# Plus-only weight sums, two of them by an accumulating DMA, and more pieces with seven block products

## The chip, the cores and the metric

One NeuronCore of a Trainium2 chip runs the kernel in one launch. The metric is device time in microseconds (us), the median of several executions; less is better.

## What is computed

One decoder layer on 256 tokens, model width 2048, all in float32. The change lies in the last stage, a dense SwiGLU network with 5632 hidden columns, and in the weights' preparation for it. Cut to that stage, the reference is:

```python
D_MODEL, SEQ = 2048, 256
D_FF = ((8 * D_MODEL // 3 + 255) // 256) * 256      # 5632
...
h2 = _rms(x, norm2_g[l])
a = jax.nn.silu(jnp.einsum('bsd,df->bsf', h2, w_gate[l])) * jnp.einsum('bsd,df->bsf', h2, w_up[l])
x = x + jnp.einsum('bsf,fd->bsd', a, w_down[l])
...
return _rms(x, final_norm_g)
```

Ahead of it stand an RMS norm, a wide projection, a spatial gate and a retention on its columns, and an output projection; none of these is changed, except that the sums of `h2` (below) are made while the output projection runs.

## The kernel before

**Three products for one.** Every float32 operand of a matrix product is split into a rounded part `hi` and the rest `lo`, and a product is made as hi·hi + hi·lo + lo·hi: three matmuls of 128x128 by 128x512 on TensorE (PE), all recorded at line 45. For the weights the split is made on the fly (`split`, lines 47 to 55): ScalarE (ACT) casts `hi` (L53), then VectorE (DVE) subtracts to get `lo` (L54). `hi` and `lo` have four buffers each, 1024 columns wide; the loaded weights `raw` have three buffers of 1 MB (128 x 2048 float32), filled by SyncE's DMA queue (SP) in the order of the program.

**Pieces.** Gate and up are computed in 11 groups `j` of 512 hidden columns. A group runs through 8 pieces `p`; a piece holds 256 rows of the weights, as two halves of 128 rows, for 512 columns of gate and 512 of up. So a piece is a product of 2x2 blocks: two row blocks of tokens and two halves on the left, two halves and {gate, up} on the right. The down projection has the same form: two groups `c` of 22 pieces, with two blocks of 512 output columns in the place of gate and up. `quad` (from line 499) runs the pieces of one group.

**Classic and seven.** A classic piece makes 8 block products, 24 matmuls. A piece in `seven` makes 7 by Winograd's form of Strassen's scheme, 21 matmuls, and pays with sums: of the left blocks (`sums_of`, made once for `h2`) and of the right blocks, the weights, for each piece (`pair_seven`, from line 475). Four of the seven products have accumulators of their own, numbered 1, 5, 7 and 6, in the PSUM pool `sm`; they run through all seven-pieces of a group, and after the last one ACT and DVE combine them (`mixed`, L533 to L537), to be added to the four classic banks in `acc`. Before, `SEVEN_GU = (1, 3, 5)`: three of the 8 pieces in each group of gate and up are seven-pieces, and none in down.

**Sums of weights.** A raw tile holds the four blocks b12, b11, b22, b21 beside each other. Before, DVE makes b12-b11 and b12-b22 in one instruction of 1024 columns (L484), then b22 minus the first (L487) and b21 minus that (L488). ACT and DVE then split four tiles: `plain` (b11, b22), `one` (the two differences), `last` (b21, 512 columns) and `two` (the other two sums).

**What sets the order.** Each engine runs its instructions in order. The order on an engine is made when the program is built, from the written order, the buffers and estimated durations; it can stand apart from the written one by some instructions. A buffer comes free when its last reader is done: a `raw` buffer with the last `lo` or sum made from it, a `hi` or `lo` buffer with the last matmul that reads it. `finish_up` (from line 575) adds banks and sums, and applies the gate (L582, L583, L587, L588); `turn_a` transposes the result on PE (L598) one group later, at the piece that `todo` names.

Of the kernel before, what the change touches and what calls it, by code (L numbers as in the profile page):

```python
# [15 lines left out]
P = 128  # L16
# [14 lines left out]
SEVEN_GU = (1, 3, 5)  # L31
# [4 lines left out]
def block_kernel(ctx: ExitStack, tc: tile.TileContext, a: dict, out: bass.AP):  # L36
# [386 lines left out]
    def sums_of(x11, x12, x21, x22, dst):  # L423

        t = ff.tile([P, 4, P], F32, name="sums", bufs=1)
        nc.vector.tensor_tensor(out=t[:, 0, :], in0=x21, in1=x22, op=ALU.add)
        nc.vector.tensor_tensor(out=t[:, 1, :], in0=x21, in1=x11, op=ALU.subtract)
        nc.vector.tensor_tensor(out=t[:, 2, :], in0=t[:, 0, :], in1=x11, op=ALU.subtract)
        nc.vector.tensor_tensor(out=t[:, 3, :], in0=x12, in1=t[:, 2, :], op=ALU.subtract)
        nc.scalar.copy(dst[:, 0, :, :], t)  # L430
        nc.vector.tensor_tensor(out=dst[:, 1, :, :], in0=t, in1=dst[:, 0, :, :].bitcast(F32), op=ALU.subtract)

    def turn_x(c):
        for half in range(2):
# [41 lines left out]
    def pair_seven(src):  # L476
# [3 lines left out]
        b12, b22, b21 = raw[:, 0:NC], raw[:, 2 * NC:3 * NC], raw[:, 3 * NC:]  # L480
        t = big.tile([P, 4 * NC], F32, name=f"mT{next(odd) % 2}")
        t13, t24 = t[:, 0:2 * NC], t[:, 2 * NC:]
        (plain,) = split(raw[:, NC:3 * NC], 2 * NC, 2 * NC)
        nc.vector.tensor_tensor(  # L484
            out=t13.rearrange("p (b c) -> p b c", b=2), in0=b12.unsqueeze(1).broadcast_to([P, 2, NC]),
            in1=raw[:, NC:3 * NC].rearrange("p (b c) -> p b c", b=2), op=ALU.subtract)
        nc.vector.tensor_tensor(out=t24[:, 0:NC], in0=b22, in1=t13[:, 0:NC], op=ALU.subtract)  # L487
        nc.vector.tensor_tensor(out=t24[:, NC:], in0=b21, in1=t24[:, 0:NC], op=ALU.subtract)  # L488
        (one,) = split(t13, 2 * NC, 2 * NC)
        (last,) = split(b21, NC, NC)  # L490
        (two,) = split(t24, 2 * NC, 2 * NC)
# [12 lines left out]
    def quad(src, order, seven, left, forms, todo=(), apart=0):  # L504
# [6 lines left out]
        classic_left = [p for p in order if p not in seven]  # L511
# [240 lines left out]
```

## Time and profile before

| | |
|---|---|
| median of 3 executions | 1107.33 us (1106.61 to 1108.31) |
| the profiled execution, its own time | 1108.35 us |
| its span, first to last instruction | 1106.1 us |
| PE busy | 1088.6 us, 98% |
| DVE busy | 810.6 us, 73% |
| ACT busy | 570.2 us, 52% |
| POOL (GpSimd) busy | 55.0 us, 5% |
| moved by DMA | 217.64 MB, 197 GB/s over the span |

An engine's busy time is the time in which it had an instruction running; an instruction's duration includes its pipeline, so that two that follow each other overlap, and the distance from one start to the next is less than the duration. A chain of waits is followed back from the last instruction to what released it. A DMA's time to landing runs from its issue to its semaphore.

### The profile page before, as it was taken

What the parts mean: (1) busy time and instruction counts of PE and PEld (TensorE: products, weight loads), DVE (VectorE), ACT (ScalarE), POOL (GpSimd) and SP (SyncE); (2) the same over time, 40 slices, a digit from 0 to 9 for tenths busy, and PEclk for the clock granted to TensorE, in tenths of its full rate; (3) what the DMA queues carried; (4) which work ended last, traced back from release to release, by engine and by line L of the source; (5) the groups of instructions that cost most, each with busy time, mean ns of one, the idle gap of its engine ahead of it and who ended that gap; (6) DMA issues with size and microseconds to landing.
All of it is one profiled execution on the core that took longest, in us unless ns stands there. A gap on an engine that the chain in (4) does not pass through costs nothing.

```text
span 1106.1 us, 12891 instructions
## 1 busy us (share of the span) xinstructions
PE 1088.6 (98%) x4937; PEld 901.6 (82%) x4937; DVE 810.6 (73%) x1097; ACT 570.2 (52%) x664; POOL 55.0 (5%) x36
## 2 busy tenths in 40 slices
PE   8989999999999999999999999999999999999996
PEld 7868888888888888888888888888888888888885
DVE  6895458466556789889898898898899555575555
ACT  6623433444445556556555555655656454454443
POOL 0051014011000000000000000000000000020000
PEclk9999999999999999999999999999999999999998
DMA  9846554545555455655645555655556655555551
GB/s 353 329 139 235 190 189 156 189 152 190 190 188 184 166 185 193 224 183 197 213 174 193 221 190 190 205 196 208 190 191 231 225 190 190 190 190 192 194 185 76
DMA packets 32749, 217.64 MB, mean 197 GB/s; under 512 B 3760, under 2 KB 4144, under 8 KB 7088
## 3 DMA queue, kind: packets, MB, share of 16 engines
q1 hardware_dynamic: 32544, 215.78, 54.7%
q0 software_dynamic: 144, 1.05, 0.3%
q8 instruction: 38, 0.62, 0.2%
q14 instruction: 23, 0.19, 0.0%
HBM read 214.72 MB, written 2.10 MB: 196 GB/s over the span
## 4 chain that ended last, share of the span: by engine, by line
PE 95%; DVE 2%; DMA 1%; ACT 0%; SPq 0%; issue 0%; DVEq 0%; ACTq 0%
PE acc L45 84%; PE sm L45 9%; PE sm L598 1%; DMA raw<-in_w_in 1%; DVE lo L54 1%; PE sm L439 0%; PE sm L334 0%; ACT junk L218 0%; DVE rs_r L75 0%; DVE rs_w L74 0%; PE sm L380 0%; DVE work L254 0%; DVE x L653 0%; SPq L168 0%; DVE rs_w L73 0%
## 5 line engine op out<-in xcount | busy, mean ns | idle before, releaser
L45 PE MATMUL acc<-hi,hT 128*128 128x512 f32 x2484 | 786.6, 391 | 1.9 <-ACT hi L53 1.9
L54 DVE TENSOR_TENSOR lo<-raw,hi 128x1024 fp32r<-128x1024 f32 (+1 forms) x396 | 463.2, 1182 | 249.6 <-ACT hi L53 243.1
L53 ACT CAST hi<-raw 128x1024 fp32r<-128x1024 f32 (+1 forms) x396 | 395.5, 1009 | 441.0 <-PE acc L45 417.5
L45 PEld LDWEIGHTS acc<-hi,hT 128*128 128x128 f32 x2484 | 467.3, 188 | 98.4 <-ACT hi L53 2.3
L45 PE MATMUL acc<-lo,hT 128*128 128x512 f32 x1242 | 484.7, 390 | 4.1 <-DVE lo L54 4.1
L45 PEld LDWEIGHTS acc<-lo,hT 128*128 128x128 f32 x1242 | 233.7, 188 | 53.3 <-DVE lo L54 5.8
L54 DVE TENSOR_TENSOR lo<-mT,hi 128x1024 fp32r<-128x1024 f32 x66 | 80.6, 1220 | 16.1 <-ACT hi L53 16.1
L53 ACT CAST hi<-mT 128x1024 fp32r<-128x1024 f32 x66 | 69.6, 1055 | 30.3 <-DVE lo L54 17.0
L45 PE MATMUL acc<-hi,mT 128*128 128x512 f32 x256 | 80.1, 391 | 0.1
L45 PE MATMUL sm<-hi,h2s 128*128 128x512 f32 x198 | 71.8, 390 | 0.0
L45 PEld LDWEIGHTS acc<-hi,mT 128*128 128x128 f32 x256 | 48.1, 188 | 10.3 <-ACT mT L383 0.5
L45 PE MATMUL acc<-lo,mT 128*128 128x512 f32 x128 | 49.7, 389 | 0.0
L45 PEld LDWEIGHTS sm<-hi,h2s 128*128 128x128 f32 x198 | 37.1, 188 | 7.7
L484 DVE TENSOR_TENSOR mT<-raw 128x1024 f32<-128x1024 f32 x33 | 40.2, 1220 | 0.8 <-DMA raw<-in_w_gu 0.2
L45 PE MATMUL sm<-lo,h2s 128*128 128x512 f32 x99 | 38.5, 389 | 0.0
L619 POOL DMA_DIRECT2D hT<-in_gf x1 | 0.7, 717 | 598.9 <-DVE mT L582 598.9
L587 ACT ACTIVATE sg<-mT,rstd 128x512 f32<-128x512 f32 x22 | 15.9, 722 | 24.6 <-DVE mT L582 24.6
L631 DVE TENSOR_TENSOR hT<-af,hT 128x1024 fp32r<-128x1024 f32 x22 | 27.9, 1267 | 0.7 <-ACT hT L630 0.7
L45 PEld LDWEIGHTS acc<-lo,mT 128*128 128x128 f32 x128 | 24.0, 188 | 4.8
L45 PE MATMUL sm<-hi,hT 128*128 128x512 f32 x66 | 25.7, 389 | 0.0
L45 PE MATMUL acc<-hi,h2s 128*128 128x512 f32 x66 | 25.7, 389 | 0.0
L258 POOL TENSOR_TENSOR work<-work,gains 128x512 f32<-128x512 f32 x8 | 17.5, 2192 | 124.1 <-DVE work L254 62.1
(99 smaller groups left out, 551.8 us busy)
## 6 DMA issues: line engine op xcount, KB each, us to landing
raw<-in_w_gu SPq DMA_DIRECT2D x88, 1024.0 KB, 4.7
raw<-in_w_in SPq DMA_DIRECT2D x47, 1024.0 KB, 4.8
raw<-in_w_down SPq DMA_DIRECT2D x44, 1024.0 KB, 4.7
raw<-in_w_out SPq DMA_DIRECT2D x16, 1024.0 KB, 4.8
x<-in_x SPq DMA_DIRECT2D x2, 1024.0 KB, 9.2
gains<-in_gains SPq DMA_DIRECT2D x2, 1024.0 KB, 6.5
out<-x SPq DMA_DIRECT2D x8, 256.0 KB, 2.5
work<-in_xT SPq DMA_DIRECT2D x7, 256.0 KB, 8.6
```

The lines of the kernel that those rows point to most:

```text
L45: nc.tensor.matmul(o, lhsT=l, rhs=r, start=start, stop=stop)
L53: nc.scalar.copy(hi, src[:, c:c + step])
L54: nc.vector.tensor_tensor(out=lo, in0=src[:, c:c + step], in1=hi.bitcast(F32), op=ALU.subtract)
L258: nc.gpsimd.tensor_tensor(out=dst, in0=dst, in1=gains[gi][:, 0, cs], op=ALU.mult)
L484: nc.vector.tensor_tensor(out=t13.rearrange("p (b c) -> p b c", b=2), in0=b12.unsqueeze(1).broadcast_to([P, 2, NC]), in1=raw[:, NC:3 * NC] ...
L587: nc.scalar.activation(sg, g, AF.Silu, scale=rstd2[r])
L598: nc.tensor.transpose(ps[:, q * S + n * P:q * S + (n + 1) * P], rows[n][:, f * P:(f + 1) * P], ident)
L619: nc.gpsimd.dma_start(gf, a["gf"].partition_broadcast(P))
L631: nc.vector.tensor_tensor(out=lo, in0=af[j], in1=hi.bitcast(F32), op=ALU.subtract)
```

## The change

In a seven-piece ACT copies b11 and b22 into a tile (line 483 of the changed kernel), and a DMA issued by POOL adds b12 to both, straight from HBM, in place (L484): 128 x 2 x 512 float32, 512 KB into SBUF, the same 256 KB of HBM read twice. DVE then makes the other two sums as plain additions (L494, L495). So that every weight sum is a plus, the signs move to the left sums (`sums_of`) and to the last addition for up (`finish_up`). Both are begun one piece ahead (`begin_seven` for piece i+1 stands ahead of piece i), and raw tiles are loaded in that order. There are more seven-pieces: 1, 3, 4 and 6 of gate and up (3, 4 and 6 in the first group), and 2, 6, 10, 14 and 18 in each group of down, whose left sums are made from `af` as they come up. The order of the products in a piece, and the places of the transposes, change too. In the first group of down the transposes of the last hidden columns go behind piece 18.

```diff
-SEVEN_GU = (1, 3, 5)
+SEVEN_GU = (1, 3, 4, 6)
+SEVEN_DOWN = (2, 6, 10, 14, 18)
...
     def sums_of(x11, x12, x21, x22, dst):
...
-        nc.vector.tensor_tensor(out=t[:, 0, :], in0=x21, in1=x22, op=ALU.add)
-        nc.vector.tensor_tensor(out=t[:, 1, :], in0=x21, in1=x11, op=ALU.subtract)
-        nc.vector.tensor_tensor(out=t[:, 2, :], in0=t[:, 0, :], in1=x11, op=ALU.subtract)
-        nc.vector.tensor_tensor(out=t[:, 3, :], in0=x12, in1=t[:, 2, :], op=ALU.subtract)
+        nc.vector.tensor_tensor(out=t[:, 0, :], in0=x22, in1=x21, op=ALU.subtract)
+        nc.vector.tensor_tensor(out=t[:, 1, :], in0=x11, in1=x21, op=ALU.subtract)
+        nc.vector.scalar_tensor_tensor(
+            out=t[:, 2, :], in0=t[:, 0, :], scalar=-1.0, in1=x11, op0=ALU.mult, op1=ALU.subtract)
+        nc.vector.tensor_tensor(out=t[:, 3, :], in0=x12, in1=t[:, 2, :], op=ALU.add)
...
-    def pair_seven(src):
+    def begin_seven(src):
 
         raw = wp.tile([P, 2048], F32, name="raw", bufs=3)
         nc.sync.dma_start(raw, src)
-        b12, b22, b21 = raw[:, 0:NC], raw[:, 2 * NC:3 * NC], raw[:, 3 * NC:]
-        t = big.tile([P, 4 * NC], F32, name=f"mT{next(odd) % 2}")
-        t13, t24 = t[:, 0:2 * NC], t[:, 2 * NC:]
+        t = big.tile([P, 4, NC], F32, name=f"mT{next(odd) % 2}")
+        nc.scalar.copy(t[:, 0:2, :], raw[:, NC:3 * NC].rearrange("p (b c) -> p b c", b=2))
+        nc.gpsimd.dma_start(t[:, 0:2, :], src[:, 0:NC].unsqueeze(1).broadcast_to([P, 2, NC]), accum_op=ALU.add)
+        return raw, t
+
+    def pair_seven(raw, t):
+
+        t = t.rearrange("p b c -> p (b c)")
+        b22, b21 = raw[:, 2 * NC:3 * NC], raw[:, 3 * NC:]
+        t1, t2, t4 = t[:, 0:NC], t[:, 2 * NC:3 * NC], t[:, 3 * NC:]
         (plain,) = split(raw[:, NC:3 * NC], 2 * NC, 2 * NC)
-        nc.vector.tensor_tensor(
-            out=t13.rearrange("p (b c) -> p b c", b=2), in0=b12.unsqueeze(1).broadcast_to([P, 2, NC]),
-            in1=raw[:, NC:3 * NC].rearrange("p (b c) -> p b c", b=2), op=ALU.subtract)
-        nc.vector.tensor_tensor(out=t24[:, 0:NC], in0=b22, in1=t13[:, 0:NC], op=ALU.subtract)
-        nc.vector.tensor_tensor(out=t24[:, NC:], in0=b21, in1=t24[:, 0:NC], op=ALU.subtract)
-        (one,) = split(t13, 2 * NC, 2 * NC)
         (last,) = split(b21, NC, NC)
-        (two,) = split(t24, 2 * NC, 2 * NC)
+        nc.vector.tensor_tensor(out=t2, in0=b22, in1=t1, op=ALU.add)
+        nc.vector.tensor_tensor(out=t4, in0=b21, in1=t2, op=ALU.add)
+        (one,) = split(t[:, 0:2 * NC], 2 * NC, 2 * NC)
+        (two,) = split(t[:, 2 * NC:], 2 * NC, 2 * NC)
...
         for i, p in enumerate(order):
+            if i + 1 < len(order) and order[i + 1] in seven:
+                ahead[order[i + 1]] = begin_seven(src(order[i + 1]))
...
-                right = pair_seven(src(p))
-                for k in (1, 3, 5, 7, 2, 6, 4) if i else (1, 5, 7, 6, 3, 2, 4):
+                right = pair_seven(*ahead.pop(p))
+                for k in (1, 3, 2, 5, 7, 6, 4):
...
-                nc.vector.tensor_tensor(out=us, in0=u, in1=us, op=ALU.add)
+                nc.vector.tensor_tensor(out=us, in0=u, in1=us, op=ALU.subtract)
...
-            todo[5] = [lambda: turn_x(3), norm2]
+            todo[2] = [lambda: turn_x(3), norm2]
         else:
-            todo[6] = [waiting]
-        bank, mixed = quad(lambda p: a["w_gu"][j, p], range(KD // 2), SEVEN_GU, h2_left, h2_forms, todo)
+            todo[7] = [waiting]
+        bank, mixed = quad(lambda p: a["w_gu"][j, p], range(KD // 2), SEVEN_GU[0 if j else 1:], h2_left, h2_forms, todo)
...
+    def a_forms(left):
...
+            if p not in made:
+                made[p] = ff.tile([P, 2, 4, P], F32R, name=f"h2s{SEVEN_GU[len(made) % len(SEVEN_GU)]}")
+                q = 2 * p % 4
+                x0, x1 = af[p // 2][:, q, :], af[p // 2][:, q + 1, :]
+                sums_of(x0[:, 0:P], x1[:, 0:P], x0[:, P:], x1[:, P:], made[p])
...
     for c in range(2):
-        todo = {6: [waiting]} if c == 0 else {}
-        bank, _ = quad(lambda p: a["w_down"][c, p], range(KF // 2), (), a_split(), None, todo, 2 if c else 0)
+        todo = {7: [waiting]} if c == 0 else {}
+        left = a_split()
+        bank, mixed = quad(
+            lambda p: a["w_down"][c, p], range(KF // 2), SEVEN_DOWN, left, a_forms(left), todo, 2 if c else 0)
+        for n in range(NT):
+            for m in range(2):
+                xs = x_sb[n][:, (2 * c + m) * NC:(2 * c + m + 1) * NC]
+                nc.vector.tensor_tensor(
+                    out=xs, in0=xs, in1=mixed[f"{n + 1}{m + 1}"], op=ALU.subtract if m else ALU.add)
```

How the change moves instructions is shown at two places, in a group of gate and up in the middle of the stage (the pattern repeats from group to group).

The first is DVE around the first seven-piece of a group, piece 1. Before (raw_4968 is piece 1, raw_5011 piece 2, raw_5045 piece 3; mT1_4970 and mT0_5047 hold the sums of pieces 1 and 3):

```order
L54 TENSOR_TENSOR lo_4979<-mT1_4970,hi_4978 128x1024
L484 TENSOR_TENSOR mT0_5047<-raw_5045 128x1024
L54 TENSOR_TENSOR lo_4983<-raw_4968,hi_4982 128x512
L487 TENSOR_TENSOR mT0_5047<-raw_5045,mT0_5047 128x512
L54 TENSOR_TENSOR lo_4987<-mT1_4970,hi_4986 128x1024
L488 TENSOR_TENSOR mT0_5047<-raw_5045,mT0_5047 128x512
L54 TENSOR_TENSOR lo_5014<-raw_5011,hi_5013 128x1024
L54 TENSOR_TENSOR lo_5018<-raw_5011,hi_5017 128x1024
```

The same place now (raw_5005 is piece 0, raw_5000 piece 1, raw_5083 piece 2, raw_5078 piece 3; mT1_5002 and mT0_5080 hold the sums of pieces 1 and 3):

```order
L55 TENSOR_TENSOR lo_5012<-raw_5005,hi_5011 128x1024
L55 TENSOR_TENSOR lo_5040<-raw_5000,hi_5039 128x1024
L55 TENSOR_TENSOR lo_5044<-raw_5000,hi_5043 128x512
L494 TENSOR_TENSOR mT1_5002<-raw_5000,mT1_5002 128x512
L55 TENSOR_TENSOR lo_5050<-mT1_5002,hi_5049 128x1024
L495 TENSOR_TENSOR mT1_5002<-raw_5000,mT1_5002 128x512
L494 TENSOR_TENSOR mT0_5080<-raw_5078,mT0_5080 128x512
L495 TENSOR_TENSOR mT0_5080<-raw_5078,mT0_5080 128x512
L55 TENSOR_TENSOR lo_5054<-mT1_5002,hi_5053 128x1024
L55 TENSOR_TENSOR lo_5086<-raw_5083,hi_5085 128x1024
```

Both additions for piece 3, which now need that piece's accumulating DMA, stand ahead of the `lo` of piece 1's `two` (lo_5054) and of piece 2.

The second is SP's queue of weight loads over the first pieces of a group. Before, pieces 0, 1, 2, 3, 4 in that order:

```order
L60 DMA raw_4934<-in_w_gu 128x2048
L479 DMA raw_4968<-in_w_gu 128x2048
L60 DMA raw_5011<-in_w_gu 128x2048
L479 DMA raw_5045<-in_w_gu 128x2048
L60 DMA raw_5088<-in_w_gu 128x2048
```

Now pieces 1, 0, 3, 2, 4, 6, 5:

```order
L481 DMA raw_5000<-in_w_gu 128x2048
L61 DMA raw_5005<-in_w_gu 128x2048
L481 DMA raw_5078<-in_w_gu 128x2048
L61 DMA raw_5083<-in_w_gu 128x2048
L481 DMA raw_5117<-in_w_gu 128x2048
L481 DMA raw_5200<-in_w_gu 128x2048
L61 DMA raw_5205<-in_w_gu 128x2048
```

With three buffers in rotation, piece 2's load now takes the buffer that piece 0 had, where before it took that of the piece ahead of piece 0.

## Rows read from the trace of the kernel before

**Rows 1.** The page: span, busy time of the engines, and the chain of waits by engine.

```profile
span 1106.1 us, 12891 instructions
...
PE 1088.6 (98%) x4937; PEld 901.6 (82%) x4937; DVE 810.6 (73%) x1097; ACT 570.2 (52%) x664; POOL 55.0 (5%) x36
...
PE 95%; DVE 2%; DMA 1%; ACT 0%; SPq 0%; issue 0%; DVEq 0%; ACTq 0%
```

**Rows 2.** Stretches: us; busy PE, PEld, DVE, ACT, POOL; granted clock, DMA share, GB/s.

```profile
632.90:675.30 42.40, 42.40 (x192) 35.02 (x192) 37.15 (x42) 24.39 (x27) 0.00 (x0) 1.00 0.56 198
...
860.00:975.00 115.00, 115.00 (x513) 95.30 (x512) 64.09 (x54) 55.76 (x59) 0.69 (x1) 1.00 0.55 194
```

**Rows 3.** Pieces of the chain of waits: start us, length us, what.

```profile
888.00 0.88 PE sm L598 x8
888.87 200.66 PE acc L45 x885
```

**Rows 4.** Groups by line and form: busy us, mean ns of one, idle before and releaser.

```profile
L54 DVE TENSOR_TENSOR lo<-raw,hi 128x1024 fp32r<-128x1024 f32 x355 | 435.2, 1239 | 213.9 <-ACT hi L53 207.5
L53 ACT CAST hi<-raw 128x1024 fp32r<-128x1024 f32 x355 | 370.3, 1053 | 347.7 <-PE acc L45 327.2 <-PE sm L45 9.2 <-DVE lo L54 5.4
...
L484 DVE TENSOR_TENSOR mT<-raw 128x1024 f32<-128x1024 f32 x33 | 40.2, 1220 | 0.8 <-DMA raw<-in_w_gu 0.2
...
L587 ACT ACTIVATE sg<-mT,rstd 128x512 f32<-128x512 f32 x22 | 15.9, 722 | 24.6 <-DVE mT L582 24.6
...
L53 ACT CAST hi<-raw 128x512 fp32r<-128x512 f32 x41 | 25.2, 622 | 93.4 <-PE acc L45 90.3 <-DMA raw<-in_w_in 3.1
```

**Rows 5.** Who waited for whom: us in total, times, longest us.

```profile
ACT hi L53 <- PE acc L45: 430.1, 287, 5.2
```

**Rows 6.** Timeline of DVE at the end of a group: start us, us, instruction.

```profile
597.85 0.68 DVE L582 TENSOR_TENSOR mT<-acc,mT 128x512 f32<-128x512 f32 x1
598.46 0.68 DVE L583 TENSOR_TENSOR mT<-acc,mT 128x512 f32<-128x512 f32 x1
...
599.65 0.75 DVE L588 SCALAR_TENSOR_TENSOR mT<-mT,rstd,sg 128x512 f32<-128x512 f32 x1
600.31 0.68 DVE L582 TENSOR_TENSOR mT<-acc,mT 128x512 f32<-128x512 f32 x1
...
601.51 1.21 DVE L54 TENSOR_TENSOR lo<-raw,hi 128x1024 fp32r<-128x1024 f32 x1
602.64 0.74 DVE L588 SCALAR_TENSOR_TENSOR mT<-mT,rstd,sg 128x512 f32<-128x512 f32 x1
```

**Rows 7.** DMA issues: KB each, median us from issue to landing.

```profile
raw<-in_w_gu SPq DMA_DIRECT2D x88, 1024.0 KB, 4.7
...
hT<-in_gf POOLq DMA_DIRECT2D x1, 1024.0 KB, 5.1
const<-in_wsT SPq DMA_DIRECT2D x1, 512.0 KB, 5.7
...
const<-in_decay SPq DMA_DIRECT2D x1, 512.0 KB, 3.2
```

**Rows 8.** Timeline of SP's queue: two of those issues with the loads beside them.

```profile
42.55 0.33 SPq L60 DMA_DIRECT2D raw<-in_w_in  x1
42.93 0.42 SPq L203 DMA_DIRECT2D const<-in_wsT  x1
...
106.86 0.33 SPq L214 DMA_DIRECT2D const<-in_decay  x1
109.66 0.33 SPq L60 DMA_DIRECT2D raw<-in_w_in  x1
```

**Rows 9.** Timeline of POOL and of DVE where POOL issues its one DMA.

```profile
855.65 0.72 POOL L619 DMA_DIRECT2D hT<-in_gf  x1 [598.91 <-DVE mT L582]
...
854.71 0.69 DVE L582 TENSOR_TENSOR mT<-acc,mT 128x512 f32<-128x512 f32 x1 [0.30 <-PE acc L45]
855.32 1.22 DVE L54 TENSOR_TENSOR lo<-raw,hi 128x1024 fp32r<-128x1024 f32 x1
```

More of the change, by code (lines that the diff above doesn't have):

```diff
@@ L423, in sums_of @@
     def sums_of(x11, x12, x21, x22, dst):
-        t = ff.tile([P, 4, P], F32, name="sums", bufs=1)
-        nc.vector.tensor_tensor(out=t[:, 0, :], in0=x21, in1=x22, op=ALU.add)
-        nc.vector.tensor_tensor(out=t[:, 1, :], in0=x21, in1=x11, op=ALU.subtract)
-        nc.vector.tensor_tensor(out=t[:, 2, :], in0=t[:, 0, :], in1=x11, op=ALU.subtract)
-        nc.vector.tensor_tensor(out=t[:, 3, :], in0=x12, in1=t[:, 2, :], op=ALU.subtract)
+        t = ff.tile([P, 4, P], F32, name="sg", bufs=2)
+        nc.vector.tensor_tensor(out=t[:, 0, :], in0=x22, in1=x21, op=ALU.subtract)
[3 more added lines that the diff above has]
+        nc.vector.tensor_tensor(out=t[:, 3, :], in0=x12, in1=t[:, 2, :], op=ALU.add)
         nc.scalar.copy(dst[:, 0, :, :], t)
@@ L450, in turn_x @@
             if p in SEVEN_GU:
-                hf = ff.tile([P, 2, S], F32, name="hf", bufs=1)
+                hf = ff.tile([P, 2, S], F32, name="sg", bufs=2)
                 for j in range(2):
@@ L510, in quad @@
         last7 = max([i for i, p in enumerate(order) if p in seven], default=-1)
-        classic_left = [p for p in order if p not in seven]
         if seven:
@@ L519, in go @@
             begun.add(b)
-        kept = []
+        kept, ahead = [], {}
         for i, p in enumerate(order):
+            if i + 1 < len(order) and order[i + 1] in seven:
+                ahead[order[i + 1]] = begin_seven(src(order[i + 1]))
             for f in todo.get(i, ()):
@@ L635, in a_split, with forms @@
         return left_of(at)
-    for c in range(2):
-        todo = {6: [waiting]} if c == 0 else {}
-        bank, _ = quad(lambda p: a["w_down"][c, p], range(KF // 2), (), a_split(), None, todo, 2 if c else 0)
+    def a_forms(left):
+        made = {}
+        def forms(p, k):
+            if k in (1, 2, 4):
+                return left(p, {1: "11", 2: "12", 4: "22"}[k])
+            if p not in made:
[3 more added lines that the diff above has]
+                sums_of(x0[:, 0:P], x1[:, 0:P], x0[:, P:], x1[:, P:], made[p])
+            j = {5: 0, 7: 1, 6: 2, 3: 3}[k]
+            return made[p][:, 0, j, :], made[p][:, 1, j, :]
+        return forms
+    for c in range(2):
+        todo = {7: [waiting]} if c == 0 else {}
[7 more added lines that the diff above has]
+                    out=xs, in0=xs, in1=mixed[f"{n + 1}{m + 1}"], op=ALU.subtract if m else ALU.add)
         for n in range(NT):
```

## Prediction

> **What bounds the kernel now.** I read the page first, then the stretches, the chain, the waits and two timelines. The page says that TensorE (PE) is busy for 98% of the span and holds 95% of the chain [rows 1]: what counts is TensorE's work, and every wait that is put into it. The stretches show the same from group to group: in a group of gate and up, 42.40 us long, TensorE is busy throughout at the full granted clock, VectorE (DVE) for 37.15 us and ScalarE (ACT) for 24.39; in down DVE is busy for 64 of 115 us, ACT for 56 [rows 2]. A matmul of 512 columns costs 200.66/885 = 0.2267 us of the chain, the 8 transposes of a group 0.88 [rows 3]; 183 matmuls and the transposes make 42.37, so a group holds no wait to speak of. The longest wait is ACT's for TensorE, 430 us in all [rows 5]: the casts stand ready and wait for buffers. DVE is the engine with little room, 12% in gate and up.
>
> **Part 1, fewer matmuls.** A seven-piece has 21 matmuls instead of 24. In gate and up, groups 1 to 10 get one seven-piece more, 30 matmuls; in down 5 in each of two groups, 30. 60 x 0.2267 = **13.6 us less**, all on the path.
>
> **Part 2, the weight sums.** In each group DVE loses three subtractions of 1024 columns at line 484 [rows 4], at a distance of 1.14 us (601.51 to 602.64, [rows 6]), 3.4 us. A fourth seven-piece instead of a classic one adds three splits of 1024 columns, one of 512 and two additions (3.4 + 0.6 + 1.2 = 5.2; a 512-column addition has a distance of 0.61) against 2.3: 2.9 more. So 37.15 - 3.4 + 2.9 = 36.7 of 41.7 us, 88% as before. ACT gets four copies of 1.05 and 1.7 for the other split [rows 4]: 24.4 + 5.9 = 30.3 of 41.7. Neither becomes the bound on average. POOL issues 53 DMAs, at 0.72 us each [rows 9] 38 us, on an engine that is idle there. Left sums: at most six instructions of 0.61 for a set on DVE, ten sets in down, 37 us beside two times 51 free ones in stretches of 115; combining the banks comes before the last pieces of a group and has the same cover. The transposes behind piece 18 are the same eight; the second four wait for ACT's copy of the first. That is 0 to 1 us once, and I take 0, as 4 matmuls stand between.
>
> **Part 3, the wait for the accumulating DMA.** This decides. Call L the time from the end of ACT's copy until the sums have landed. I work out what DVE and TensorE allow at three places, with the distances above, casts of 1.05 and 0.62, and the gate's activation of 0.72 [rows 4, 6].
>
> *Place A, pieces 0 to 2.* Let 0 be the end of piece 6 on TensorE. Transposes and piece 7 take 6.3, piece 0 ends at 11.8. DVE can add the last bank at 6.6 (0.30 after the product, [rows 9]), ends it at 7.2 and the two gate products (0.66 each, [rows 6]) at 8.5, and makes the `lo` of piece 0's second half by 9.7; only then may piece 2's load be issued. ACT ends the second activation at 7.2, the cast of `last` at 7.9, the copy for piece 3 at 8.9. DVE goes on: `plain` 10.8, `last` 11.4, a sum 12.0, `one` 13.2, a sum 13.8. Next in its order stand both additions of piece 3, so L may be 13.8 - 8.9 = 4.9. Behind them (1.2) stands the `lo` of piece 1's `two`, ready at 16.1; TensorE wants it as its 20th matmul of piece 1, at 11.8 + 19 x 0.2267 = 16.1. There is nothing to spare: all of L over 4.9 stalls TensorE. Besides, ACT casts `two` at 13.8 to 14.9 and the first half of piece 2 until 15.9, while TensorE's order has a product of it 18th, at 15.6: 0.3 even with a fast DMA. A = max(0.3, L - 4.9), in 10 groups; the first has no seven-piece there.
>
> *Place B, pieces 3 and 4.* ACT's casts go on (16.9, 18.0, 18.6) and the copy for piece 4 ends at 19.65; its load, issued at 13.8, lands at 18.5 (4.7, [rows 7]). TensorE starts piece 3 at 11.8 + 0.3 + 45 x 0.2267 = 22.3 and wants the `lo` of its `two` at 25.9; ahead of that DVE needs an addition and the `lo`, 1.75. So the sums must be there at 24.15, and L may be 4.5. B = max(0, L - 4.5), in 11 groups.
>
> *Place C, down.* ACT's copy for a seven-piece (take 14) stands behind the cast of piece 12's second half, which needs the buffer of piece 10's `two`: it ends 2.2 us after TensorE's end of piece 10. TensorE starts piece 13 at 10.9 and wants its `lo` 0.2 later; DVE first makes two additions (1.2), a left block's `lo` and the piece's own (1.14 each). 11.1 - 3.5 - 2.2 leaves L = 5.4. C = max(0, L - 5.4), for 8 seven-pieces; the first of each group is begun far ahead.
>
> *L itself* no row shows; no DMA adds here before. 512 KB land in 3.2 us where no load is near (next one 2.8 us later) and in 5.7 when issued 0.4 us behind a 1 MB load [rows 7, 8]. POOL's 1 MB took 5.1, SP's 4.7 [rows 7]: 0.4 more. So the lower end is 3.6, the upper 5.7 + 0.4 = 6.1. Reading the destination as well may make 512 KB as long as 1 MB: 5.1, between the ends. At A piece 2's load comes 0.8 us behind the DMA, not ahead of it, so it is nearer to the free row than to the other; I take **4.7**. Then A is 10 x 0.3 = 3.0, B 11 x 0.2 = 2.2, C nothing: **5.2 us more**.
>
> The Trainium skill ("DMA: Bandwidth & Descriptors", Anatomy of one DMA) fits such a DMA as 2.0 us plus bytes over 436 GB/s, 3.2 us for 512 KB, by which only A's 0.3 is left and the median would be 1096.7. The same fit gives 4.4 for the 1 MB that took 5.1 [rows 7], so here it is short.
>
> **Sum.** -13.6 + 5.2 = -8.4. The profiled execution took 1108.35 us, 2.25 more than its span; 1108.35 - 8.4 = 1099.95. The median lies 1.0 below that execution: **1099.0 us**. With L at its lower end it is 1096.7, without A's 0.3 as well 1093.7; with L = 6.1 the waits are 12.0 + 17.6 + 5.6 = 35.2, and the median is 1128.9.
>
> **Rivals.** *Slower: the loads and the sums share the DMA engines.* The place is A and B; the price per us of L is 10 + 11 (and 8 in down); from L of 5.4 on the waits eat the 13.6. With L = 5.7 they are 8.0 + 13.2 + 2.4 = 23.6: **1117.3**. For it: the row of 5.7 [rows 8], a DMA share of 56% in a group [rows 2], piece 2's load right behind the DMA, piece 6's load in flight at B. Against it: the DMA is issued first, and the load of a piece takes 4.7 of some 5.2 us, so that it leaves gaps.
>
> *All of it is hidden.* L of 3.6 or less, and A's 0.3 absorbed, since the durations I summed are means: 1093.7 to 1096.7. For it: ACT waits 430 us for TensorE [rows 5], so its part of the chains has room. Against it: DVE has none at A.
>
> *POOL is held off by DVE.* If a `lo` with two inputs in SBUF kept POOL from issuing, L would grow by up to one `lo`, 1.24 [rows 4], to 5.9: waits 10.0 + 15.4 + 4.0 = 29.4, median 1123.2. POOL's one DMA before began 0.33 us into such a `lo` and took 0.72, while the `lo` took its usual 1.22 [rows 9], so it was not held. The Trainium skill ("SBUF — State Buffer", SBUF: two separate sides) says that VectorE and GpSimd lock a shared port pair for a whole instruction and that a POOL-issued DMA can starve so; it limits that to other VectorE operations than these, and row and page agree.
>
> *The change does less than it says* is excluded: the built program has 60 matmuls of 512 columns fewer.
>
> **How the numbers follow.** A measurement of this kernel can tell about 0.2% (2.2 us) from no change: 1105.1 to 1109.5. Faster by more needs L under 5.2, slower by more L over 5.45. The forecast (L from 3.8 to 5.2; own range 1096.7 to 1105) gets 0.37, all hidden 0.20, the narrow case between 0.10, sharing DMA engines 0.29, a held POOL 0.04. So faster 0.57, same 0.10, slower 0.33. Range: from 1093.5, the full 13.6, to 1121, which is L = 5.8; beyond lie about 0.15.
>
> **What would show it.** Right: 60 matmuls fewer; a group of 42.0 to 42.3 us; DVE's first addition of a seven-piece (L494) waits for POOL's DMA only briefly; POOL's DMA lands in about 4.5. Wrong: TensorE idle before a `lo` of `two` or a `hi` of the piece behind, 1 us and more in each group, with DVE waiting at L494 (L over 5.4); or piece 2's cast waiting for its load. If TensorE waits at other places than A and B, the chains are wrong, not only L.

## The result, and the profile after

The changed kernel takes **1288.83 us** (median of 4 executions, 1285.06 to 1290.58) against 1107.73 us before (4 executions): ratio 1.1634, 95% interval 1.1617 to 1.1651. It is 16% slower where 0.8% faster was forecast.

The page of the changed kernel, span and busy time, TensorE's granted clock in 40 slices, and the DMA queues (packets, MB, share of 16 engines' span):

```profile
span 1288.8 us, 13175 instructions
...
PE 1148.2 (89%) x4877; PEld 927.1 (72%) x4877; DVE 860.3 (67%) x1215; ACT 646.6 (50%) x772; POOL 120.2 (9%) x89
...
PEclk9999999999999989889899897988989889999998
...
q1 hardware_dynamic: 32544, 215.78, 47.5%
q0 software_dynamic: 14560, 28.84, 12.7%
```

The 60 matmuls are gone (4877 against 4937 in [rows 1]), and yet TensorE is busy for 59.6 us longer. Three terms make up the 182.7 us between the spans. TensorE's idle time went from 1106.1 - 1088.6 = 17.5 to 1288.8 - 1148.2 = 140.6 us: **123.1 us of new stalls**. Its work took 59.6 us longer although 13.6 us of it had been removed: **73.2 us of slower matmuls**, and the clock row, which before is 9 in all slices but the last, now falls to 8, once to 7, again and again from the 15th slice on. And **-13.6**: 123.1 + 73.2 - 13.6 = 182.7.

By stage, the first and the last activation of the gate bound ten groups (one line of each kernel, its instructions: count, duration in ns, first and last start in us; L587 before, L594 after):

```profile
L587 ACT ACTIVATE sg<-mT,rstd x22: 713/722/727, 428.3 to 856.4; 128x512 f32<-128x512 f32 x22
```

```profile
L594 ACT ACTIVATE sg<-mT,rstd x22: 707/713/720, 439.9 to 988.3; 128x512 f32<-128x512 f32 x22
```

So 11.6 us were lost up to the first gate, 548.4 - 428.1 = 120.3 in ten groups, and 300.5 - 249.7 = 50.8 behind the last one.

Where TensorE stands in one group, the timeline of the changed kernel (only the instructions of ACT's copy, ACT's cast of piece 2, POOL, piece 2's load on SP, DVE's first addition and those of TensorE that waited):

```profile
604.91 1.05 ACT L483 COPY mT<-raw 128x1024 f32<-128x1024 f32 x1
606.26 1.20 POOL L484 DMA_DIRECT2D mT<-in_w_gu  x1 [11.66 <-ACT mT L483]
606.79 0.33 SPq L61 DMA_DIRECT2D raw<-in_w_gu  x1
612.66 2.94 ACT L54 CAST hi<-raw 128x1024 fp32r<-128x1024 f32 x3 [0.70 <-DMA raw<-in_w_gu]
613.76 0.73 PE L46 MATMUL acc<-hi,hT 128*128 128x512 f32 x2 [0.79 <-ACT hi L54]
615.62 0.69 DVE L494 TENSOR_TENSOR mT<-raw,mT 128x512 f32<-128x512 f32 x1 [4.82 <-DMA mT<-in_w_gu]
618.23 0.80 PE L46 MATMUL sm<-lo,h2s 128*128 128x512 f32 x1 [3.74 <-DVE lo L55]
620.87 1.05 ACT L483 COPY mT<-raw 128x1024 f32<-128x1024 f32 x1
622.22 1.20 POOL L484 DMA_DIRECT2D mT<-in_w_gu  x1 [14.76 <-ACT mT L483]
632.10 0.69 DVE L494 TENSOR_TENSOR mT<-raw,mT 128x512 f32<-128x512 f32 x1 [5.33 <-DMA mT<-in_w_gu]
633.98 0.79 PE L46 MATMUL sm<-lo,h2s 128*128 128x512 f32 x1 [4.57 <-DVE lo L55]
```

These are places A and B of the prediction. At A the wait for `hi` of piece 2 (0.79) and for `lo` of piece 1's `two` (3.74) make 4.5 us; at B it is 4.6. The first of the two waits has a cause of its own: ACT's cast of piece 2 waited 0.70 us for piece 2's load. Place C, the same in down:

```profile
1035.42 1.05 ACT L483 COPY mT<-raw 128x1024 f32<-128x1024 f32 x1
1036.77 1.20 POOL L484 DMA_DIRECT2D mT<-in_w_down  x1 [29.29 <-DVE lo L55]
1047.06 0.69 DVE L494 TENSOR_TENSOR mT<-raw,mT 128x512 f32<-128x512 f32 x1 [7.68 <-DMA mT<-in_w_down]
1050.80 0.80 PE L46 MATMUL acc<-lo,hT 128*128 128x512 f32 x1 [5.28 <-DVE lo L55]
```

The time L from the end of ACT's copy until DVE can go on is 615.62 - 605.96 = 9.7 us at A, 10.2 at B and 10.6 at C (medians over all groups: 9.2, 10.0 and 9.7), where 4.7 had been taken. The DMA as a whole (issues of L484: KB each, median us to landing):

```profile
mT<-in_w_gu POOLq DMA_DIRECT2D x43, 512.0 KB, 8.8
mT<-in_w_down POOLq DMA_DIRECT2D x10, 512.0 KB, 9.4
```

and over all 53 (min, median, max):

```profile
DMA to landing us min/median/max: 5.3/9.0/10.8
```

By the trace's packets the short ones (5.3 to 6.0) are those of piece 1, with little of a load beside them, and two single ones (the last of gate and up, the first in the second group of down). Beside the others, of pieces 3, 4 and 6 and of down, 1 to 2 MB of loads are moved.

What the stalls do to the clock (stretches of the group above; columns as in [rows 2], the granted clock third from the end):

```profile
597.00:612.96 15.96, 15.96 (x74) 12.82 (x72) 13.49 (x18) 8.42 (x12) 1.20 (x1) 1.00 0.59 163
612.96:617.70 4.74, 0.74 (x3) 0.30 (x2) 2.05 (x3) 2.64 (x3) 0.00 (x0) 1.00 0.86 279
617.70:621.10 3.40, 2.87 (x7) 2.29 (x8) 3.40 (x4) 0.76 (x2) 0.00 (x0) 0.50 0.00 0
621.10:629.40 8.30, 8.30 (x37) 6.52 (x35) 2.31 (x3) 4.49 (x5) 1.20 (x1) 1.00 0.93 286
629.40:631.40 2.00, 0.01 (x1) 0.00 (x0) 0.00 (x0) 0.00 (x0) 0.00 (x0) 0.99 0.70 126
631.40:638.20 6.80, 4.22 (x10) 3.35 (x11) 5.91 (x7) 3.04 (x3) 1.20 (x1) 0.50 0.14 18
638.20:652.40 14.20, 14.20 (x63) 11.41 (x63) 9.68 (x10) 9.32 (x11) 1.20 (x1) 1.00 0.88 268
```

With each of the two stalls the granted clock falls to 0.50, that is 1.2 instead of 2.4 GHz, for 3.4 and 6.8 us (the second time while TensorE still waits). In the last stage there are 28 such stretches, 143 us in all, one behind each of the 29 stalls (10 at A, 11 at B, 8 at C) but the last of B, of 1.3 us. TensorE is at work in 120 of the 143 us; half of that, 60 us, is what the half clock costs, the larger part of the 73. The rest was not followed up; a part of it is that the last matmul ahead of a stall counts with its whole duration (0.39 us) and not with the distance to the next.

### The profile page after: what moved, and what is told of

Its sections match the earlier page's. It is cut to its first block, busy times and chain, and to the rows that moved or that the text cites. A ratio compares the mean times of both kernels' runs of the same rounds, so it can differ in the third digit from the quotient of the medians.

```text
span 1288.8 us, 13175 instructions
## 1 busy us (share of the span) xinstructions
PE 1148.2 (89%) x4877; PEld 927.1 (72%) x4877; DVE 860.3 (67%) x1215; ACT 646.6 (50%) x772; POOL 120.2 (9%) x89
## 3 DMA queue, kind: packets, MB, share of 16 engines
q1 hardware_dynamic: 32544, 215.78, 47.5%
q0 software_dynamic: 14560, 28.84, 12.7%
## 5 line engine op out<-in xcount | busy, mean ns | idle before, releaser
L46 PE MATMUL acc<-hi,hT 128*128 128x512 f32 x2244 | 746.5, 404 | 9.0 <-ACT hi L54 8.7
L46 PEld LDWEIGHTS acc<-hi,hT 128*128 128x128 f32 x2244 | 440.3, 197 | 108.1 <-ACT hi L54 13.8
L54 ACT CAST hi<-mT 128x1024 fp32r<-128x1024 f32 x106 | 111.1, 1049 | 198.1 <-PE acc L46 153.8
L55 DVE TENSOR_TENSOR lo<-mT,hi 128x1024 fp32r<-128x1024 f32 x106 | 129.7, 1223 | 101.2 <-ACT hi L54 100.1
L494 DVE TENSOR_TENSOR mT<-raw,mT 128x512 f32<-128x512 f32 x53 | 37.3, 704 | 165.4 <-DMA mT<-in_w_gu 100.6
L46 PE MATMUL sm<-lo,h2s 128*128 128x512 f32 x159 | 70.5, 444 | 68.9 <-DVE lo L55 68.7
L46 PE MATMUL sm<-hi,h2s 128*128 128x512 f32 x318 | 113.2, 409 | 5.5 <-ACT hi L54 5.5
L484 POOL DMA_DIRECT2D mT<-in_w_gu x43 | 51.9, 1207 | 655.1 <-ACT mT L483 358.0
L46 PEld LDWEIGHTS sm<-lo,h2s 128*128 128x128 f32 x159 | 31.7, 199 | 85.3 <-DVE lo L55 79.8
L483 ACT COPY mT<-raw 128x1024 f32<-128x1024 f32 x53 | 55.5, 1047 | 49.1 <-DVE lo L55 39.9
L495 DVE TENSOR_TENSOR mT<-raw,mT 128x512 f32<-128x512 f32 x53 | 37.5, 708 | 1.0
L484 POOL DMA_DIRECT2D mT<-in_w_down x10 | 12.0, 1197 | 245.2 <-DVE lo L55 140.5
```

What stands on the lines that cost most here:

```text
L46: nc.tensor.matmul(o, lhsT=l, rhs=r, start=start, stop=stop)
L54: nc.scalar.copy(hi, src[:, c:c + step])
L55: nc.vector.tensor_tensor(out=lo, in0=src[:, c:c + step], in1=hi.bitcast(F32), op=ALU.subtract)
L483: nc.scalar.copy(t[:, 0:2, :], raw[:, NC:3 * NC].rearrange("p (b c) -> p b c", b=2))
L484: nc.gpsimd.dma_start(t[:, 0:2, :], src[:, 0:NC].unsqueeze(1).broadcast_to([P, 2, NC]), accum_op=ALU.add)
L494: nc.vector.tensor_tensor(out=t2, in0=b22, in1=t1, op=ALU.add)
```

## Experiments

The theory after the result: the accumulating DMA lands late beside the loads; DVE, which works in order, waits for it in front of a `lo` that TensorE needs; TensorE stalls, and its clock falls behind each stall. Rivals: the rest of the change costs the time; the DMA is slow by itself, not by the loads; the clock falls for another reason.

**No DMA: VectorE adds (e1_dve).** In `begin_seven`:

```diff
-        nc.scalar.copy(t[:, 0:2, :], raw[:, NC:3 * NC].rearrange("p (b c) -> p b c", b=2))
-        nc.gpsimd.dma_start(t[:, 0:2, :], src[:, 0:NC].unsqueeze(1).broadcast_to([P, 2, NC]), accum_op=ALU.add)
+        nc.vector.tensor_tensor(
+            out=t[:, 0:2, :], in0=raw[:, 0:NC].unsqueeze(1).broadcast_to([P, 2, NC]),
+            in1=raw[:, NC:3 * NC].rearrange("p (b c) -> p b c", b=2), op=ALU.add)
```

> Theory (the accumulating DMA and the clock): all of the loss comes from VectorE waiting in its order for the DMA of line 484, which takes 5.1 us alone and 8.4 to 9.6 beside a 1 MB load, from TensorE's stalls behind it, and from the half clock after each stall. With one VectorE addition of 1024 columns in place of ACT's copy and the DMA there is nothing to wait for: 1093 to 1103 us, granted clock 0.99 or more, the upper part because VectorE then has 36.7 + 4 x 1.14 = 41.2 us of work in a group of 41.7. Rival (the rest of the change: one piece ahead, order of loads, order of products, left sums in down): it costs with or without the DMA, so over 1150 us.

Measured: 1108.14 us (10 executions), ratio to before 1.0006 (0.9994 to 1.0019). All of the loss is gone with the DMA (and ACT's copy for it), so the rest of the change does not cause it. But it lies 5 us above the range, and the 13.6 us don't appear either. A group:

```profile
635.00:677.40 42.40, 42.24 (x189) 34.37 (x188) 41.08 (x47) 25.10 (x30) 0.00 (x0) 1.00 0.57 199
```

DVE is busy for 41.08 of 42.40 us where it was 37.15 before [rows 2]: TensorE's 41.7 us of work now wait, a little at a time, for DVE. And behind the last gate it takes 249.8 us like the kernel before, with a stall of 2.0 us at the start of down, for a load.

**GpSimd adds (e2_pool).** The same line with `nc.gpsimd` in place of `nc.vector`.

> The two sums as one addition of 1024 columns on GpSimd in place of ACT's copy and the DMA. GpSimd's additions of 512 columns took 1.66 to 2.19 us before, so one of 1024 takes 3.3 to 4.4. Theory (the accumulating DMA and the clock): that is inside the 4.5 to 5.4 us that the three places allow, so 1094 to 1105 us. If GpSimd and VectorE hold each other up when both read SBUF, the addition or the lo next to it gets longer by more than 0.5 us and the stalls come back in part: 1110 to 1180. Rival (the rest of the change): over 1150 with the stalls at the same places though the sums are early.

Measured: 1173.96 us, ratio 1.0604 (1.058 to 1.0628): the second of the three cases. By line and form:

```profile
L483 POOL TENSOR_TENSOR mT<-raw 128x1024 f32<-128x1024 f32 x53 | 173.7, 3277 | 674.3 <-DMA raw<-in_w_gu 398.5 <-DVE lo L55 120.7 <-DMA raw<-in_w_down 116.8
L55 DVE TENSOR_TENSOR lo<-raw,hi 128x512 fp32r<-128x512 f32 x61 | 65.7, 1081 | 3.5 <-ACT hi L54 3.4
```

An addition takes 3.28 us, at the lower end of what was expected, but a `lo` of 512 columns takes 1081 ns in the mean where it took 687 in the changed kernel. DVE is busy for 907.2 us; without its own 53 additions the kernel of e1 has 914.3 - 64.6 = 849.7. So each addition on GpSimd costs DVE (907.2 - 849.7) / 53 = 1.1 us of busy time, about what DVE needs to make it. By the durations of DVE's other instructions, added up without regard to their overlap, it is 50.8 us in all, 0.96 for each. DVE also waits 49.8 us for GpSimd. The Trainium skill ("SBUF — State Buffer", Who interferes with whom) says that a VectorE operation of two SBUF inputs and a GpSimd operation that reads SBUF hold each other up; the 1081 against 687 ns agree.

**No seven-pieces in down (e3_no_down).** `SEVEN_DOWN = ()`, and with it the additions of the seven-pieces' sums behind down.

> No seven-pieces in down; gate and up as in the changed kernel. Theory: the 8 stalls of down (4.3 to 5.4 us each, 37.6 in sum) and the half clock behind them (34 us of it, worth 17) go, 30 matmuls (6.8 us) come back: 1288.8 - 37.6 - 17 + 6.8 = 1241 us, and down as long as before. Rival (stalls in down come from the left sums or from the queue of loads that the groups before leave behind): the same number, but then with the stalls of gate and up changed too; a time over 1260 would speak for it.

Measured: 1241.23 us (one execution). Behind the last gate it takes 1239.5 - 989.8 = 249.7 us, the same as before, and ten groups take 549.9. So the two stages add up, and the 17 us put down for the half clock behind C fit.

**Fill the stalls with work (e4_fill).** In `three`, with 16, 18 or 20 for the three places:

```diff
         mm(bank, lh, rh, start, False)
+        for _ in range(fill):
+            mm(bank, zero, rh, False, False)
```

> 518 matmuls with a stationary tile of zeros (16, 18 and 20 of them, 3.6 to 4.5 us) stand where TensorE stalls: behind the first matmul of the product with two in pieces 1 and 3 of gate and up, and behind the first matmul of the piece ahead of a seven-piece in down. They add zero to a bank that is open; the result is the same, the work is 117 us more. Theory (TensorE's idle time is what lowers its clock): the wait is then filled, the clock stays at 0.98 or more, and the 73 us that the half clock costs come back: 1205 to 1235 us with MORE work. Rival (the clock falls for another reason, such as the DMA traffic or the work done so far): 1280 us or more, and half-clock stretches at the same places.

Measured: 1335.5 us (one execution), 46.7 slower instead of 54 to 84 faster. The 117.4 us of added work changed DVE's order: at B the wait moved to an earlier `lo`, ahead of the fill, and stalls of up to 6.6 us came up there and elsewhere. Idle time fell by 42.0 us (98.6 against 140.6), and TensorE's busy time rose by 86.9 us, not by 117.4: 30.5 us came back from the clock. As a whole a miss, and by its time alone the rival would hold. But the half-clock stretches of the last stage went from 28 (143 us) to 13 (68 us). What it tells best is in down, where in its second group three fills stand where the stalls were. First the changed kernel, two of TensorE's waiting matmuls (a round of four pieces lies between two of them):

```profile
1166.33 0.50 PE L46 MATMUL acc<-lo,hT 128*128 128x512 f32 x1 [4.37 <-DVE lo L55]
1194.42 0.68 PE L46 MATMUL acc<-lo,hT 128*128 128x512 f32 x1 [5.06 <-DVE lo L55]
```

and two such rounds as stretches:

```profile
1166.90:1194.30 27.40, 22.46 (x92) 17.99 (x90) 13.97 (x15) 12.43 (x13) 1.20 (x1) 0.94 0.55 173
1194.30:1222.00 27.70, 23.25 (x94) 18.74 (x95) 15.03 (x16) 12.42 (x13) 1.20 (x1) 0.94 0.53 171
```

The same in the filled kernel, first two of the fills:

```profile
1096.29 4.74 PE L46 MATMUL acc<-hi,zero 128*128 128x512 f32 x20
1121.99 4.74 PE L46 MATMUL acc<-hi,zero 128*128 128x512 f32 x20
```

and the two rounds:

```profile
1096.30:1122.00 25.70, 25.70 (x115) 21.19 (x114) 16.16 (x20) 13.07 (x15) 1.20 (x1) 1.00 0.56 184
1122.00:1147.70 25.70, 25.70 (x115) 21.19 (x114) 16.15 (x20) 13.07 (x15) 1.20 (x1) 1.00 0.56 184
```

With 20 matmuls more a round is 25.70 instead of 27.4 to 27.7 us, at clock 1.00 instead of 0.94. The DMA traffic is no less (share 0.56 against 0.53 to 0.55). So in these rounds the clock fell with the idle time, and not with the traffic or the work done. The price of filling all places is more than the clock gives back.

**The DMA only where no stall stood behind it (e5_hybrid).** `begin_seven` gets a flag: DMA for pieces 1 and 6 of gate and up, DVE's addition elsewhere.

> The accumulating DMA only for pieces 1 and 6 of gate and up, where the changed kernel showed no stall behind it; VectorE's addition for pieces 3 and 4 and for all of down. Theory: in the kernel with VectorE's additions alone a group took 42.40 us with VectorE busy for 41.08, so VectorE was the bound there; without two additions it has 41.1 - 2 x 1.14 = 38.8 us of work, TensorE sets the group again (180 matmuls and 8 transposes, 41.7 us), and 10 groups save 0.7 each: 1108.1 - 7 = 1099 to 1102 us. Rival (a DMA that lands late hurts anywhere, since VectorE's additions for it stand in its queue): a group of 44 us and more, stalls of TensorE in front of pieces 1 or 6, over 1110 us.

Measured: 1127.95 us, ratio 1.0172 (1.0149 to 1.0194): a miss; the rival holds. A group as a stretch:

```profile
560.60:605.00 44.40, 42.96 (x190) 34.19 (x189) 39.12 (x46) 26.64 (x32) 2.41 (x2) 1.00 0.68 214
```

and DVE's wait for the DMA (us in all, times, longest):

```profile
DVE mT L499 <- DMA mT<-in_w_gu: 22.0, 11, 3.0
```

DVE waits 2 us in each group for piece 6's DMA, which lands in 7.1 to 8.9 us, and behind that wait TensorE stands still for up to 1.5 us a group, for a `hi` and a `lo` of piece 6. By the sums alone DVE would have these 2 us (39.1 + 2.0 of 41.7); what they cost comes from where they stand in its order. In the changed kernel DVE came to piece 6's sum just as the DMA landed, 9.2 us behind ACT's copy (median). The likely reason, not tested by itself, is that TensorE, and DVE behind it, had already been held up at A and B. Room that is seen in a kernel full of stalls need not be room.

**The same DMA without the addition (e6_plain).** `accum_op=ALU.add` is taken away; the order of every engine is the same.

> The same DMA without the accumulation: it writes b12 twice over ACT's copy, so b11 and b22 are left out of the sums; every engine's order is the same, instruction for instruction. Theory 1 (the adding itself is slow): a 2 KB packet took 178 ns in the adding DMA and 84 ns in plain ones, 16 packets an engine, so the DMA gets 1.5 us shorter: 3.6 us alone, 7.0 beside a load; 29 stalls are 1.5 shorter each and their half-clock stretches shorter with them: 1288.8 - 44 - 10 to 30 = 1215 to 1235. Theory 2 (it is only the queue behind the load): the first packet still comes 5.2 us after the issue and the time changes by less than 20 us.

Measured: 1242.77 us (one execution), 46 less, 8 above the range of theory 1 and far from theory 2. The DMAs (min, median, max):

```profile
DMA to landing us min/median/max: 4.1/6.6/9.9
```

The median is 2.4 us shorter, not 1.5: besides the packets the issue on POOL takes 0.72 instead of 1.20 us. But the places differ (medians): 1.3 us shorter with no load beside it (piece 1, 5.4 to 4.1), 1.0 at B (9.7 to 8.7) and 1.2 in down (9.4 to 8.2), and 2.3 at A (8.9 to 6.6) and 2.6 in piece 6. More than the adding has changed, for POOL's queue has about half the packets for the same bytes (14560 above):

```profile
q0 software_dynamic: 7776, 28.84, 7.9%
```

And at A the DMA's first packet now comes 1.4 us after the issue and ahead of the load's, not after 5.2 us and behind some 121 of the load's 128. So the adding by itself is worth 1.0 to 1.3 us; the rest of the 2.4 goes with the turns that its packets and the loads' take. Stalls remain at all three places. At B and in down that is since beside loads even the plain DMA is too slow. At A the stall left is mostly another wait, that of ACT's cast of piece 2 for its own load: 1.2 to 1.9 us in each of ten groups, since that load takes 6.3 to 7.7 us beside the DMA. One of them:

```profile
602.59 2.95 ACT L54 CAST hi<-raw 128x1024 fp32r<-128x1024 f32 x3 [1.29 <-DMA raw<-in_w_gu]
```

**Lighter loads beside the DMA (e7_light).** A classic piece loads 512 KB instead of 1 MB:

```diff
-        return load_piece(src)
+        raw = wp.tile([P, 2048], F32, name="raw", bufs=3)
+        nc.sync.dma_start(raw[:, 0:1024], src[:, 0:1024])
+        return split(raw[:, 0:1024], 1024, 1024) + split(raw[:, 0:1024], 1024, 1024)
```

> Classic pieces load half of their weights (512 KB instead of 1 MB) and use that half twice; the other half is left out of the computation. Theory 2 (the DMA shares the 16 engines with the load beside it): the DMA beside a load lands about 1.7 us earlier (8.5 becomes 6.8, in down 9.1 becomes 7), 29 stalls get that much shorter, and with the half clock behind them the time falls to 1200 to 1235 us. Theory 1 (the adding itself): the DMA stays at 8.4 to 9.6 us and the time within 15 us of 1288.

Measured: 1207.49 us (one execution), within theory 2's range. The DMAs:

```profile
DMA to landing us min/median/max: 5.3/7.8/9.6
```

In down the last packet now comes 6.1 to 7.6 us after the issue instead of 9.0 to 10.4 (the first DMA of the second group aside, which has little beside it), and only waits of 0.6 us are left there; in gate and up A and B keep stalls of 1.1 to 3.6 us. So both theories hold a part: without the adding the DMA is 2.4 us shorter of 9 (1.0 to 1.3 by the adding itself), with half a load beside it 1.2 in the median and some 2 in down, and with no load at all, as at piece 1 of the changed kernel, 3.3 to 4.2. The stalls of down, 4.3 to 5.4 us long, went altogether, which is more than these 2 us explain; what else the lighter loads moved was not followed up.

**GpSimd makes the two additions behind the DMA (e8_pooladd).** Lines 494 and 495 with `nc.gpsimd`.

> The two additions behind the DMA (lines 494, 495) are made by GpSimd instead of VectorE, so that no instruction of VectorE waits for the DMA ahead of a lo that TensorE needs. Theory (the wait becomes a stall only through VectorE's order): with the same 8.5 to 9.6 us DMA, piece 3's sums come in time in spite of 3.3 us of additions, and so do those of down, so the stalls at places A and C go (about 40 + 38 us idle and some 40 us of half clock); piece 4's come about 4 us late and B stays: 1150 to 1200 us. Rival (TensorE waits for the DMA's own data): stalls at all three places as before, 1270 us or more.

Measured: 1179.17 us (one execution), in the middle of the range. The DMA is hardly faster:

```profile
DMA to landing us min/median/max: 5.3/8.3/12.0
```

and now POOL waits for it:

```profile
POOL mT L494 <- DMA mT<-in_w_gu: 286.9, 43, 10.9
POOL mT L494 <- DMA mT<-in_w_down: 80.4, 10, 10.4
```

Behind the last gate it takes 1177.4 - 930.5 = 246.9 us, less than the kernel before, with DMAs of up to 12 us: where DVE doesn't wait, the DMA is hidden in down. What remains in gate and up (49.9 us a group) is B, where TensorE now waits for the late sums of piece 4 themselves, and that POOL issues one DMA in most groups 6 to 8 us late, since it stands behind the additions.

**Three seven-pieces and down (e9_three); the DMA for piece 1 alone (e10_dma1); more seven-pieces in down (e11_three7).** e9 is e1 with `SEVEN_GU = (1, 3, 5)` in all groups; e10 is e5 with the DMA for piece 1 only; e11 is e9 with `SEVEN_DOWN = (2, 4, 7, 10, 13, 15, 18)`.

> No accumulating DMA; seven-pieces 1, 3 and 5 in gate and up as in the kernel before, with the sums by VectorE, and the five of down. Theory (VectorE bounds a group of four seven-pieces without the DMA; in down it has room): a group as before, 42.4 to 42.5 us, and down 246 to 247 us where the kernel before took 252.3 from the last transposes of gate and up, as with VectorE's sums in all of it: 1107.5 - 6 = 1101 to 1103 us. Rival (down gains nothing by itself either, the 5.8 us were an effect of the other groups): 1106 to 1109.

> Four seven-pieces in gate and up; the accumulating DMA for piece 1 alone, whose DMA landed in 5.0 to 5.1 us in every run, with no load beside it; VectorE's addition elsewhere. Theory (VectorE's room decides): VectorE has 41.1 - 1.14 = 40.0 us of work and waits for no DMA, so a group takes 41.7 to 42.0 us and the time is 1108.1 - 10 x 0.4 to 0.7 = 1101 to 1104 us. Rival (the DMA costs wherever it is, by its issue or by its share of the DMA engines): a group over 42.4 and 1108 us or more.

> As the run with three seven-pieces in gate and up and no DMA, with seven instead of five seven-pieces in each group of down (2, 4, 7, 10, 13, 15, 18). Each saves 3 matmuls (0.68 us) and costs VectorE some 5 us of sums and splits where it had 89 of 115 us: 4 x 0.68 = 2.7 us less than that run if VectorE has the room, 1098 to 1101; if seven-pieces two pieces apart crowd VectorE, no gain or a loss: 1102 to 1106.

Measured: e9 1102.48 us, ratio 0.9943 (0.993 to 0.9957); e10 1103.35, 0.996 (0.9945 to 0.9975); e11 1100.89, 0.9934 (0.9921 to 0.9947). All three times lie in the ranges of the theory. A group of e9:

```profile
638.10:680.50 42.40, 42.40 (x193) 35.19 (x192) 37.50 (x42) 24.50 (x28) 0.00 (x0) 1.00 0.55 198
```

A group of e10:

```profile
633.10:675.10 42.00, 42.00 (x190) 34.35 (x189) 40.10 (x46) 26.19 (x31) 1.20 (x1) 1.00 0.66 213
```

its DMA:

```profile
mT<-in_w_gu POOLq DMA_DIRECT2D x10, 512.0 KB, 9.3
```

and a stretch of down in e11:

```profile
900.00:1015.00 115.00, 114.65 (x508) 93.82 (x507) 113.03 (x141) 73.53 (x87) 7.43 (x4) 1.00 0.56 198
```

Two of the grounds were not right. The expectation of e9 took the length of down from the last transposes, which stand one piece later in the changed kernel. From the last gate, e9 takes 1101.9 - 857.6 = 244.3 us against 249.7: 5.4 of the 6.8 us, where e1 gained nothing; the stall of 2.0 us at the start of down, which e9 doesn't have, is a part of that difference, and the rest is open. And piece 1's DMA in e10 takes 9.3 us, not 5.1 (in the changed kernel 5.1 to its last packet, 5.3 to 5.8 to its landing): it now stands beside a load. DVE doesn't wait for it all the same, since its turn comes 10.9 us behind ACT's copy, some 1.3 us after the landing. In e11 DVE is busy for 113.0 of 115 us: more seven-pieces have no room there.

**Both (e12_both).** e10 with the seven seven-pieces of e11 in down.

> The two versions together: four seven-pieces in gate and up with the DMA for piece 1 alone, and seven seven-pieces in down. Their gains lie in different stages (groups of 42.0 instead of 42.4 us; down 1.6 us shorter than with five), so by the theory that VectorE's room decides they add up: 1107.9 - 4.5 - 1.6 = 1100 to 1102 us by the medians, or 1097 to 1100 if the shortest runs are the measure. Rival (each gives back what the other gains, where the stages meet): 1103 or more.

Measured: 1100.18 us, ratio 0.9938 (0.9924 to 0.9953): in the range, at its lower end, and not to be told from e11. The two gains do not add up fully: behind the last gate it takes 1097.5 - 851.3 = 246.2 us against e11's 1099.0 - 856.1 = 242.9. e11 and e12 are faster than the kernel before by 0.7 and 0.6%.

## Why the prediction was wrong

**The matmuls.** Right: 60 fewer, none in dispute.

**The places.** Right: 29 stalls, at A, B and C, and nothing over 0.8 us elsewhere in the last stage, mainly for the reasons given. With the L that was measured (9.7, 10.2, 10.6) the formulas give 4.8, 5.7 and 5.2 us; the rows show 4.5, 4.6 and 5.3. What the sum lacked at A is the load of piece 2: beside the DMA it takes 5.5 to 6.5 us instead of 4.7, and ACT's cast waits for it for 0.4 to 0.8 us in nine of ten groups, one of the signs of being wrong that had been named. In the changed kernel the later wait for `lo` covers it.

**L.** This is the first step that failed: "I take 4.7", with 6.1 as the upper end. Even without a load the DMA needs 5.3, and 0.3 pass between the end of ACT's copy and its issue, so L would be 5.6 with nothing beside it, already more than A, B and C allow. The other 3.6 to 5.0 us come with the loads beside it. The rows that were used as bounds were plain DMAs. Adding makes POOL's issue 1.20 instead of 0.72 us and doubles the time on the DMA engines: in the page above 28.84 MB on POOL's queue take 12.7% (0.44% a MB), 215.78 MB of loads 47.5% (0.22% a MB); without the adding the 28.84 MB take 7.9% of a shorter span (e6). "Reading the destination as well" had been thought of, as a value between the ends; it was to be the lower end. And "the DMA is issued first" did not help: at A SP's load is issued 0.53 us behind it, and by the packets some 121 of the load's 128 went ahead of the DMA's first. The rival of shared DMA engines was the right mechanism, far too small: L of 5.7 instead of 10, and 23.6 us of waits instead of 123.1.

**The clock.** The second step, which was missing: a stall was priced at its own length. 123.1 us of idle time brought 73.2 us of slower matmuls, of which some 60 lie in the half-clock stretches, so a us of stall cost about 1.6. The stretches that were read before have a clock of 1.00 [rows 2], since TensorE hardly stood still there. But far ahead of the last stage the same trace of the kernel before shows the clock fall, behind two waits of 2 us (two instructions, then a stretch):

```profile
65.62 0.50 PE L45 MATMUL acc<-lo,hT 128*128 128x512 f32 x1 [2.09 <-DVE lo L54]
73.40 0.50 PE L45 MATMUL acc<-lo,hT 128*128 128x512 f32 x1 [2.00 <-DVE lo L54]
```

```profile
74.90:78.30 3.40, 3.40 (x9) 2.63 (x8) 2.36 (x3) 1.03 (x1) 3.16 (x1) 0.50 0.79 275
```

So that a stall costs more than its own length could have been seen, and nothing in the sum left room for it.

**Cover.** DVE's work in a group was forecast right (36.7, measured 36.8), and "Neither becomes the bound" held for the kernel as changed, but the 1093.7 to 1096.7 given for "all of it is hidden" was not to be had by taking the DMA away: with its 41.1 us DVE is the bound at 42.4 (e1). The accumulating DMA buys DVE 1.14 us a piece. It pays where it is issued long before its turn: for piece 1 (e10 against e1), not for piece 6 as well (e5). Even so e10 is not to be told from e9, which has no such DMA.

**POOL held off by DVE.** Excluded as argued: the issue began 0.3 us behind the end of ACT's copy (once 0.6) and took 1.18 to 1.33 us in all 53 cases.

## What to carry to other kernels

A DMA in the middle of a dependent chain is priced with the transfers that are in flight at that moment, and an adding DMA at twice its bytes; the instruction that waits for it must not stand in an in-order queue ahead of work that the bounding engine needs. Price a stall of TensorE above its own length, since its clock can fall behind it, here behind 28 of 29. And before an engine is given work to free another one, count the room of the freed engine in the kernel as it would run without stalls, not in a profile full of them.

## What the runs showed of the hardware that had not been expected

An accumulating DMA from HBM into SBUF takes twice the DMA engines' time of a plain one: a 2 KB packet 178 ns against 84 ns for the plain 2 KB packets of the other queue, in the same trace (medians). The same DMA without the adding has 128 packets of 4 KB at 159 ns instead of 256 at 178. The Trainium skill ("Collectives: The Full Stack", The bandwidth ceiling: the fold count and why AG ≠ RS ≠ AR) says of the additions of a ReduceScatter that they halve the rate because two sources are read, with one descriptor for each, and not because of the adding. It does not speak of a DMA into SBUF; the factor of 2.1 here agrees.

TensorE's clock: 28 stretches of 3.4 or 6.8 us at 1.2 GHz behind stalls of 2.2 to 5.5 us; where 20 matmuls of zeros stood in place of the stall, in down, there was none, and the round was 1.7 to 2.0 us shorter for 4.5 us more work.

An addition on GpSimd costs VectorE about as much of its time (1.0 to 1.1 us for 1024 columns) as VectorE would need to make it (1.14).
